# Prompt attention with plain float32 operands, two kv heads per step on halves of the TensorE array

## The chip, the cores and the metric

One core of a Trainium2 chip runs the whole program. The metric is the device time of one execution in microseconds, the median of several. The engines are TensorE (PE for its matmuls, PEld for its weight loads), VectorE (DVE), ScalarE (ACT), GpSimd (POOL) and the engine that issues most loads (SP). Each works through its own queue in order, and waits for the others by semaphores.

## What is computed

The program is a two-layer decoder step for one prompt of 512 tokens and eight short samples. The change concerns the attention of layer 1 for the prompt alone: 16 heads in 4 kv groups, 4 heads to a group, 64 numbers to a head. Each head attends three times (compressed, selected and window branch), each with its own keys and values, and the three outputs are added with gates. With 512 tokens every causal block is selected and the window holds every earlier token, so both of the last two branches are causal attention over 512 keys.

```python
s = jnp.einsum('bqgrd,bngd->bqgrn', qg, ck)                    # compressed, 31 keys
p_cmp = masked_softmax(s, cend[None, None, None, None, :] <= t5)
o_cmp = jnp.einsum('bqgrn,bngd->bqgrd', p_cmp.astype(cv.dtype), cv)
...
s = jnp.einsum('bqgrd,bqgksd->bqgrks', qg, kv_sel[..., 0, :])  # selected
p = masked_softmax(s, m.reshape(B, Q, KV_HEADS, 1, k_sel * SEL_BLOCK))
o_slc = jnp.einsum('bqgrks,bqgksd->bqgrd', p, kv_sel[..., 1, :])
s = jnp.einsum('bqgrd,bmgd->bqgrm', qg, wkv[:, :, 0])          # window
p = masked_softmax(s, wm[None, :, None, None, :])
o_win = jnp.einsum('bqgrm,bmgd->bqgrd', p.astype(wkv.dtype), wkv[:, :, 1])
o = g[..., 0:1] * o_cmp + g[..., 1:2] * o_slc + g[..., 2:3] * o_win
...
return o @ w_o, ...
```

## The kernel before

`prompt_attention` (L1318) runs between sample attention, whose last operations overlap its loads, and `out_proj` (L1558), which multiplies the outputs by `nsa_w_o`. All operands of its matmuls are in a float32 format of one pass (F32R), and accuracy is kept by splitting a number into a high and a low part.

*Operands.* Queries (`queries`, L1402) are loaded by a query head r of all four groups, split by ACT and DVE or POOL into `qhl` with high and low side by side, and transposed so that 64 rows hold the high and 64 rows the low parts (`queries2`). Keys (`load_keys`, `keys`) are loaded twice side by side, four loads a tile plus one for values, transposed, and split into `KSh`, `KSl`, `KWh`, `KWl`; a product of `[qh; ql]` with `[k; k]` over 128 rows then has both query parts. Values become `VP`, high and low as 128 columns.

*Items.* There are 32 items (r, p, e, j): r the query head of a group, group g = 2p + e, j the branch (0 selected, 1 window). `scores_step` makes the causal scores of four query tiles t with 512, 384, 256 and 128 keys, two matmuls each; DVE adds the mask and takes the minimum (L1478), ACT takes the exponential and its sum (L1479), POOL multiplies by gate over sum (L1487). Tile t=0 shares a PSUM bank with another tile. `transpose_step` turns ten 128 x 128 blocks and splits them into `pph` and `ppl` (ACT, then DVE). `values_step` does two matmuls per key tile, adds the compressed branch at j=1 (L1523) and then adds the two column halves of the result (`osum`), splits the sum into `xh` (ACT) and `xl` (POOL).

*Order.* In loop i stand scores of item i, transposes of item i-2 and values of item i-3. A table `plan` sets when a round r prepares the next: query load, transposes, compressed scores (`pk`), their softmax (`ec`) and its transposes (`pct`). The scheduler turns this into a fixed queue on each engine; PSUM has eight banks, all in one pool. `out_proj` fetches the weights in four quarters `rawb1` to `rawb4`, each in four loads of SP, splits each into `whb` (ACT, L247) and `wlb` (DVE, L248), and loads the residual `xz` on ACT's queue. Where a tile lies, and so what a load into it must wait for, is decided by the pools.

Of the kernel before, what the change touches and what calls it, by code (L numbers as in the profile page):

```python
# [20 lines left out]
TP = 512  # L21
# [31 lines left out]
LASTI = (31,)  # L53
LASTT = (0, 1, 2)
B1 = 8
PLA = 2
PB = 4
PT = 2
# [73 lines left out]
def body(tc, top, I, O):  # L132
# [1185 lines left out]
    def prompt_attention(ctx):  # L1318
        gp_ = N["gp"]
        qp = Slots(ctx, "pq", "right", kd=2, vt=2, qs=1, qhl=1)  # L1320
        pa = Slots(ctx, "pa", Q=2)
# [3 lines left out]
        kvs = []  # L1325

        def load_keys(t):
            kd = qp.tile([128, 2, 4, 2, 64], F32, tag="kd", name=f"kd{t}")
            vt = qp.tile([128, 2, 4, 64], F32, tag="vt", name=f"vt{t}")
            for j in range(2):  # L1330
                src = kvd[t * 128:(t + 1) * 128, 1 + j].rearrange("p (k g c) -> p k g c", k=2, g=4)
                for e in range(2):
                    sp.dma_start(kd[:, j, :, e], src[:, 0])
            sp.dma_start(vt.rearrange("p j g c -> p j (g c)"), kvd[t * 128:(t + 1) * 128, 1:3, 256:512])
            kvs.append((kd, vt))

        load_keys(0)
        load_keys(1)
        KS = [pa.tile([128, 4, 512], F32R, name=f"KS{n}") for n in "hl"]
        KW = [pa.tile([128, 4, 512], F32R, name=f"KW{n}") for n in "hl"]  # L1340
        VP = [pa.tile([128, 4, 4, 2, 64], F32R, name=f"VP{j}") for j in range(2)]

        KB = pa.tile([128, 2, 640], F32R, name="KB")
        pool.memset(f32(KB), 0.0)
        cvp = pa.tile([128, 4, 2, 64], F32R, name="cvp")
# [3 lines left out]
        pp.reserve("osum", 2)  # L1349
        for tag in ("pha", "pla", "phb", "plb", "phc", "plc", "pch", "pcl"):  # L1350
            ptp.reserve(tag, PT)
        pool.memset(f32(cvp), 0.0)

        def compressed():
            hs = N["hid"]
            hg_ = ptp.tile([128, TP], F32R, tag="pch", name="hgp").rearrange("p (a k n) -> p a k n", a=2, k=2)
# [6 lines left out]
            ptv = pt[:, :128].rearrange("p (g n) -> p g n", g=4)  # L1363
            kb = KB.rearrange("p a (g n) -> p a g n", g=4)[:, :, :, 0:32]
            b2k = N["b2"][:, 64:65]
            act.activation(kb[:, 0], ptv, AF.Identity, bias=b2k)
            dve.scalar_tensor_tensor(kb[:, 1], ptv, b2k, f32(kb[:, 0]), OP.add, OP.subtract)
# [5 lines left out]
            dve.tensor_tensor(cvf, pt[:, 64:128], cvf, OP.add)  # L1373
            for g in range(4):
                rs = slice(32 * g, 32 * g + 32)
                dve.tensor_copy(cvp[rs, g, 0], cvf[rs])
                dve.tensor_tensor(cvp[rs, g, 1], cvf[rs], f32(cvp[rs, g, 0]), OP.subtract)

        def keys(t):
            if t > 1:  # L1380
                load_keys(t)
            kd, vt = kvs[t]
            for j in range(2):
                pt = tpt(f"pkp{t}{j}")
                for g in range(4):
                    transpose(pt[:, g * 128:(g + 1) * 128], kd[:, j, g].rearrange("p e c -> p (e c)"))
                pv = pt.rearrange("p (g n) -> p g n", g=4)
                hi, lo = ((KS, KW)[j][n][:, :, t * 128:(t + 1) * 128] for n in range(2))
                act.activation(hi, pv, AF.Copy)
                dve.tensor_tensor(lo, pv, f32(hi), OP.subtract)  # L1390
                act.activation(VP[j][:, t, :, 0], vt[:, j], AF.Copy)
                pool.tensor_tensor(VP[j][:, t, :, 1], vt[:, j], f32(VP[j][:, t, :, 0]), OP.subtract)

        keys(0)
        keys(1)
# [7 lines left out]
        def queries(r):  # L1403

            Q[r] = pa.tile([128, 4, TP], F32R, tag="Q", name=f"Q{r}")
            qs = qp.tile([128, 4, 4, 64], F32, tag="qs", name=f"qs{r}")
            for t in range(4):
                sp.dma_start(qs[:, t], qd[t * 128:(t + 1) * 128].rearrange("p (g r c) -> r p g c", g=4, r=4)[r])
            qhl = qp.tile([128, 4, 4, 2, 64], F32, tag="qhl", name=f"qhl{r}")
            act.activation(qhl[:, :, :, 0].bitcast(F32R), qs, AF.Copy)  # L1410
            (pool if r else dve).tensor_tensor(qhl[:, :, :, 1], qs, qhl[:, :, :, 0], OP.subtract)
            gate[r] = gpv[:, :, :, r]
            return qhl

        def queries2(r, qhl):
            for g in range(4):
                pt = tpt(f"pq{r}{g}")
                for t in range(4):
                    transpose(pt[:, t * 128:(t + 1) * 128], qhl[:, t, g].rearrange("p s c -> p (s c)"))
                evac(Q[r][:, g], pt)  # L1420

        def cmp_scores(r):
            pk = mmt(f"pk{r}")
            for n in range(2):
                for g in range(4):
# [28 lines left out]
        def cmp_probs(r, ec):  # L1454
            pt = tpt(f"pct{r}")
            for t in range(4):
                transpose(pt[:, t * 128:(t + 1) * 128], ec[:, t].rearrange("p g n -> p (g n)"))
            pch = ptp.tile([128, TP], F32R, tag="pch", name=f"pch{r}")
            pcl = ptp.tile([128, TP], F32R, tag="pcl", name=f"pcl{r}")
            act.activation(pch, pt, AF.Copy)  # L1460
            dve.tensor_tensor(pcl, pt, f32(pch), OP.subtract)
            cmpp[r] = (pch, pcl)

        items = [(r, p, e, j) for r in range(4) for p in range(2) for e in range(2) for j in range(2)]
        probs, probsT, acc, osum = {}, {}, {}, {}

        def scores_step(i):
            r, p, e, j = items[i]
            g, K = 2 * p + e, (KS, KW)[j]
            P = pp.tile([128, 1280], F32, tag="P", name=f"P{i}")  # L1470
            st = sm.tile([128, 4, 4], F32, tag="st", name=f"st{i}")
            banks = [mmt(f"psp{i}{q}") for q in range(3)]
            views = [banks[1][:, 384:512], banks[2][:, 0:256], banks[1][:, 0:384], banks[0]]
            for t in (3, 2, 0, 1):
                n = (t + 1) * 128
                for hl in range(2):
                    pe.matmul(views[t], Q[r][:, g, t * 128:(t + 1) * 128], K[hl][:, g, 0:n], start=hl == 0, stop=hl == 1)  # L1477
                dve.tensor_tensor_reduce(P[:, tri(t)], views[t], pm[:, 512 - n:512], 1.0, 3e38, OP.add, OP.min, st[:, 1, t:t + 1])  # L1478
                act.activation(P[:, tri(t)], P[:, tri(t)], AF.Exp, bias=st[:, 1, t:t + 1], scale=-1.0, accum_out=st[:, 2, t:t + 1])  # L1479
            dve.reciprocal(st[:, 3], st[:, 2])  # L1480
            dve.tensor_tensor(st[:, 3], st[:, 3], gate[r][:, :, g, 1 + j], OP.mult)
            for t in (3, 2, 0, 1):
                x = P[:, tri(t)]
                if i in LASTI and t in LASTT:
                    dve.tensor_scalar(x, x, st[:, 3, t:t + 1], None, OP.mult)
                else:
                    pool.tensor_tensor(x, x, st[:, 3, t:t + 1].broadcast_to([128, (t + 1) * 128]), OP.mult)  # L1487
            probs[i] = P

        def transpose_step(i):  # L1490
            P = probs.pop(i)
            out = {}
            for name, group in (("a", ((0, 0),)), ("b", ((1, 0), (3, 384))), ("c", ((2, 0),))):
                pt = tpt(f"ppp{i}{name}")
                w = 0
                for kc, c0 in group:
                    for t in range(kc, 4):
                        w = c0 + (t - kc + 1) * 128
                        transpose(pt[:, w - 128:w], P[:, tri(t)][:, kc * 128:(kc + 1) * 128])
                ph = ptp.tile([128, 512], F32R, tag="ph" + name, name=f"pph{name}{i}")  # L1500
                pl = ptp.tile([128, 512], F32R, tag="pl" + name, name=f"ppl{name}{i}")
                act.activation(ph[:, :w], pt[:, :w], AF.Copy)
                dve.tensor_tensor(pl[:, :w], pt[:, :w], f32(ph[:, :w]), OP.subtract)
                for kc, c0 in group:
                    n = (4 - kc) * 128
                    out[kc] = (ph[:, c0:c0 + n], pl[:, c0:c0 + n])
            probsT[i] = out
# [275 lines left out]
```

## Time and profile before

| | us |
|---|---|
| median of 3 runs (1708.69 to 1710.13) | 1709.5 |
| the profiled execution | 1708.67 |
| its span, first to last instruction | 1706.9 |
| sample attention's last transpose starts | 1011.5 |
| first scores of prompt attention | 1024.6 |
| first matmul of the output projection | 1193.2 |

Times in the rows below are microseconds from the start of the span. The granted clock of TensorE over the span is 0.988 of the full level. A timeline row is one instruction, or a run of equal ones, with the idle time ahead of it and what ended that; its length includes the passage through the array, so that lengths of back-to-back matmuls overlap. In the chain of waits each piece lasts until the next one begins, and its pieces add up. A plain float32 matmul leaves two records in the trace, one of F32R one.

### The profile page before, as it was taken

Reading aid. Unit: us, or ns where it says so; the run is one execution under the profiler, and the core shown is the slowest. Engines: PE = TensorE matmul, PEld = TensorE weight load, DVE = VectorE, ACT = ScalarE, POOL = GpSimd, SP = SyncE. Lnnn points to the kernel's source line nnn. Section 1 sums busy time; section 2 is a strip of 40 time slices with the busy share of each in tenths; the row PEclk is TensorE's granted clock in tenths of the full one; section 3 lists DMA queues with packets and bytes.
Section 4 is the critical chain, followed back from the end, with each engine's and each line's share of the span. In section 5 each row is a group of like instructions: output and inputs, shape, how many; then the busy total and the mean of one; then the engine's idle time right before and its main releaser. Section 6 shows DMA issues by size and latency. Waiting matters only on the chain. (4 is left out here: it accounts for less than half of the span.)

```text
span 1706.9 us, 31668 instructions
## 1 busy us (share of the span) xinstructions
PE 1638.8 (96%) x12711; PEld 1555.0 (91%) x12711; DVE 1046.9 (61%) x2162; ACT 816.3 (48%) x1499; POOL 426.5 (25%) x606
## 2 busy tenths in 40 slices
PE   7999999999999989999999988999999999999995
PEld 7999999999999989999956667887999999999995
DVE  7766464545574347889755558898466545454547
ACT  5654334343353314655654447888256534344331
POOL 2222121111020013333312216766023202111104
PEclk9999999999999999999999999999999999999998
DMA  5233132223247736544659941002512222222211
GB/s 190 83 100 100 55 111 83 75 75 99 63 167 214 229 119 244 187 167 164 208 182 350 342 124 26 1 12 69 153 50 75 78 96 75 84 90 81 93 60 56
DMA packets 130850, 206.02 MB, mean 121 GB/s; under 512 B 25775, under 2 KB 106761, under 8 KB 120336
## 3 DMA queue, kind: packets, MB, share of 16 engines
q1 hardware_dynamic: 120800, 134.49, 25.0%
q0 software_dynamic: 9216, 67.11, 11.1%
q8 instruction: 100, 1.64, 0.4%
q10 hardware_dynamic: 688, 2.40, 0.4%
q14 instruction: 46, 0.38, 0.1%
HBM read 179.63 MB, written 24.84 MB: 120 GB/s over the span
## 5 line engine op out<-in xcount | busy, mean ns | idle before, releaser
L168 PE MATMUL u<-xl,wha 128*128 128x288 f32 x704 | 208.0, 296 | 0.3 <-POOL xl L342 0.2
L168 PE MATMUL u<-xl,whb 128*128 128x288 f32 x704 | 208.0, 296 | 0.2
L168 PE MATMUL u<-xh,whb 128*128 128x288 f32 x704 | 207.3, 295 | 0.0
L168 PE MATMUL u<-xh,wha 128*128 128x288 f32 x704 | 207.3, 295 | 0.0
L168 PE MATMUL u<-xh,wlb 128*128 128x288 f32 x704 | 207.3, 295 | 0.0
L168 PE MATMUL u<-xh,wla 128*128 128x288 f32 x704 | 207.2, 295 | 0.0
L408 POOL COPY fcol<-u 128x18 f32<-128x18 f32 x88 | 69.4, 798 | 467.1 <-ACT u L407 467.0
L413 DVE SCALAR_TENSOR_TENSOR c<-u,convp,c 128x592 f32<-128x592 f32 x88 | 72.2, 831 | 122.2 <-ACT c L412 122.2
L248 DVE TENSOR_TENSOR wla<-rawa,wha 128x2048 fp32r<-128x2048 f32 (+1 forms) x52 | 99.5, 1918 | 68.7 <-ACT wha L247 68.0
L248 DVE TENSOR_TENSOR wlb<-rawb,whb 128x2048 fp32r<-128x2048 f32 x37 | 84.8, 2292 | 83.4 <-ACT whb L247 83.4
L168 PEld LDWEIGHTS u<-xl,wha 128*128 128x128 f32 x704 | 132.0, 188 | 2.0 <-DVE xl L342 1.1
L168 PEld LDWEIGHTS u<-xl,whb 128*128 128x128 f32 x704 | 132.0, 188 | 1.9 <-DVE xl L342 1.1
L168 PEld LDWEIGHTS u<-xh,whb 128*128 128x128 f32 x704 | 132.0, 188 | 0.1
L168 PEld LDWEIGHTS u<-xh,wha 128*128 128x128 f32 x704 | 132.0, 188 | 0.1
L168 PEld LDWEIGHTS u<-xh,wlb 128*128 128x128 f32 x704 | 132.0, 188 | 0.0
L168 PEld LDWEIGHTS u<-xh,wla 128*128 128x128 f32 x704 | 132.0, 188 | 0.0
L247 ACT ACTIVATE wha<-rawa 128x2048 fp32r<-128x2048 f32 (+1 forms) x52 | 83.0, 1615 | 91.1 <-PE d L168 58.9
L247 ACT ACTIVATE whb<-rawb 128x2048 fp32r<-128x2048 f32 x37 | 70.9, 1915 | 113.5 <-DMA rawb<-in_ffn_w_up 41.0
L494 DVE SCALAR_TENSOR_TENSOR xz<-xz,d 128x288 f32<-128x288 f32 x160 | 70.1, 450 | 85.5 <-PE d L168 84.8
L901 PE MATMUL pr<-xhi,W1h 128*128 128x256 f32 x512 | 105.6, 288 | 10.2 <-ACT xhi L874 10.2
L874 ACT ACTIVATE xhi<-xf 128x1024 fp32r<-128x1024 f32 (+1 forms) x68 | 70.1, 1031 | 83.1 <-PE pr L901 46.0
L168 PE MATMUL d<-hh,wha 128*128 128x288 f32 x352 | 104.4, 298 | 0.1
(779 smaller groups left out, 4900.6 us busy)
## 6 DMA issues: line engine op xcount, KB each, us to landing
rawa<-in_ffn_w_up SPq DMA_DIRECT2D x22, 1024.0 KB
rawb<-in_ffn_w_up SPq DMA_DIRECT2D x22, 1024.0 KB
rawa<-in_ffn_w_down SPq DMA_DIRECT2D x11, 1024.0 KB
rawb<-in_ffn_w_down SPq DMA_DIRECT2D x11, 1024.0 KB
rawa<-in_nsa_w_in SPq DMA_DIRECT2D x9, 1024.0 KB
sr<-in_state_win_kv SPq DMA_DIRECT2D x8, 1024.0 KB
out_win_kv_s<-sr SPq DMA_DIRECT2D x8, 1008.0 KB
rawb<-in_nsa_w_o SPq DMA_DIRECT2D x16, 256.0 KB
```

The costliest lines, as they stand in the source:

```text
L168: pe.matmul(out, a, b, start=first and j == 0, stop=last and j == n - 1)
L247: act.activation(h[:, a:b], r[:, a:b], AF.Copy)
L248: dve.tensor_tensor(lo[:, a:b], r[:, a:b], f32(h[:, a:b]), OP.subtract)
L408: pool.tensor_copy(col[:, :, m].rearrange("p (j i) -> p j i", i=2), u[:, TP:TP + 90].rearrange("p (j i) -> p j i", i=10)[:, :, 0:2])
L413: dve.scalar_tensor_tensor(c, u[:, 1:1 + CW], cv[:, 44 + m:45 + m], c, OP.mult, OP.add)
L494: dve.scalar_tensor_tensor(z, z, ALPHA if first else 1.0, p_[:, :HALF], OP.mult, OP.add)
L874: act.activation(xhi.rearrange(flat), xf.rearrange(flat), AF.Copy)
L901: pe.matmul(banks[b, kv][ri][:, :, gh * nn:(gh + 1) * nn], W1[wi][:, kv, ri * 8 + th * 4 + c], xx[:, c // 2, c % 2].rearrange("p g n -> p ...
```

## The change

The matmuls of the attention take plain float32 operands, without parts. One step does both groups e = 0, 1 of a pair p, so there are 16 steps (r, p, j).

- Scores: keys and queries of two groups lie in the two halves of the 128 rows (`KT`, `Q`), and each group's matmul uses 64 rows, one matmul per (t, e), in different PSUM banks, six banks a step.
- Values: each group's matmul uses 64 of the array's columns and writes its half of one bank, `po`; values are read straight from the loaded tile `kvt`. The compressed branch likewise; the outputs are split from `po` itself, high part on ACT, low part on DVE.
- Compressed scores: four matmuls on quarters of the columns, instead of eight on the whole array.
- Transposes of P stay ten per item, each block copied once (DVE a, a, c; ACT b, b, c of a step).
- Loads: four whole-row loads `kvt` for keys and values, no duplicates, and no split of queries. 8 transposes of queries a round instead of 16, 16 of keys instead of 32.
- Six buffers of P instead of four, four of the transposed instead of two; one step of look-ahead. In the last step DVE and POOL share the multiplies.

The core of the diff:

```diff
-        qp = Slots(ctx, "pq", "right", kd=2, vt=2, qs=1, qhl=1)
-        pa = Slots(ctx, "pa", Q=2)
+        qp = Slots(ctx, "pq", "right", qs=2)
+        pa = Slots(ctx, "pa", QT=2)
...
+        for t in range(4):
+            x = pa.tile([128, 2, 512], F32, name=f"kvt{t}")
+            sp.dma_start(x, kvd[t * 128:(t + 1) * 128, 1:3])
+            kvt.append(x)
+        KT = pa.tile([128, 2, 2, TP], F32, name="KT")
...
         def cmp_scores(r):
             pk = mmt(f"pk{r}")
-            for n in range(2):
-                for g in range(4):
-                    pe.matmul(pk, KB[:, n, 128 * g:128 * g + 128], Q[r][:, g], start=n == 0 and g == 0, stop=n == 1 and g == 3)
+            for g in range(4):
+                pe.matmul(pk[32 * g:32 * g + 32], KB[:, g], Q[r][:, g // 2], start=True, stop=True, tile_position=(0, 32 * g))
...
         def scores_step(i):
-            r, p, e, j = items[i]
-            g, K = 2 * p + e, (KS, KW)[j]
...
-            banks = [mmt(f"psp{i}{q}") for q in range(3)]
-            views = [banks[1][:, 384:512], banks[2][:, 0:256], banks[1][:, 0:384], banks[0]]
             for t in (3, 2, 0, 1):
                 n = (t + 1) * 128
-                for hl in range(2):
-                    pe.matmul(views[t], Q[r][:, g, t * 128:(t + 1) * 128], K[hl][:, g, 0:n], start=hl == 0, stop=hl == 1)
...
+                for e in range(2):
+                    if t:
+                        bank = mmt(f"psp{i}{e}{t}")
+                        views[e, t] = bank[:, 0:n]
+                        if t == 2:
+                            views[e, 0] = bank[:, 384:512]
+                    rs = slice(64 * e, 64 * e + 64)
+                    pe.matmul(views[e, t], Q[r][rs, p, t * 128:(t + 1) * 128], KT[rs, j, p, 0:n], start=True, stop=True)
...
         def transpose_step(i):
...
-                act.activation(ph[:, :w], pt[:, :w], AF.Copy)
-                dve.tensor_tensor(pl[:, :w], pt[:, :w], f32(ph[:, :w]), OP.subtract)
+                    if name == "b" or (name == "c" and e):
+                        act.activation(ph[:, :w], pt[:, :w], AF.Copy)
+                    else:
+                        dve.tensor_copy(ph[:, :w], pt[:, :w])
...
         def values_step(i):
...
-                v = VP[j][:, kc, g].rearrange("p a c -> p (a c)")
-                for q, x in enumerate(pT[kc]):
-                    pe.matmul(po[:, kc * 128:], v, x, start=j == 0 and kc == 0 and q == 0, stop=False)
+                for e in range(2):
+                    g = 2 * p + e
+                    pe.matmul(po[64 * e:64 * e + 64, kc * 128:], kvt[kc][:, j, 256 + 64 * g:320 + 64 * g], pT[e][kc],
+                              start=j == 0 and kc == 0, stop=False)
             if j == 1:
-                act.activation(o, po[64:128], AF.Copy)
-                dve.tensor_tensor(o, po[0:64], o, OP.add)
...
+                for e in range(2):
+                    pe.matmul(po[64 * e:64 * e + 64], cvp[:, 2 * p + e], cmpp[r], start=False, stop=True)
+                act.activation(oh[:, c, 0:TP], po, AF.Copy)
+                dve.tensor_tensor(ol[:, c, 0:TP], po, f32(oh[:, c, 0:TP]), OP.subtract)
...
-        for i in range(len(items) + LA + 1):
+        for i in range(len(items) + 2):
```

*Order of PE.* Before, in the first round: `psp31` is item 3's bank for t=2 and t=0, `psp32` its bank for t=1, `ppp1` are the transposes of item 1.

```order
L1477 MATMUL psp31_12452<-KWh_12062,Q0_12196 128x384
L1477 MATMUL psp31_12452<-KWl_12066,Q0_12196 128x384
L1477 MATMUL psp32_12453<-KWh_12062,Q0_12196 128x256
L1477 MATMUL psp32_12453<-KWl_12066,Q0_12196 128x256
L1477 MATMUL psp21_12391<-KSh_12054,Q0_12196 128x128
L1477 MATMUL psp21_12391<-KSl_12058,Q0_12196 128x128
L200 MATMUL ppp1a_12476<-cst_58,P1_12344 128x128 x4
L200 MATMUL ppp1b_12485<-cst_58,P1_12344 128x128 x4
L200 MATMUL ppp1c_12494<-cst_58,P1_12344 128x128 x2
L1477 MATMUL psp31_12452<-KWh_12062,Q0_12196 128x128
L1477 MATMUL psp31_12452<-KWl_12066,Q0_12196 128x128
L200 MATMUL pct0_12501<-cst_58,ec0_12376 128x128 x4
```

Now, step 9 (`psp902`: step 9, group e=0, bank of t=2; its second row is t=0), followed by the transposes of step 8 for e=0 (`ppp80`):

```order
L1451 MATMUL psp903_13123<-KT_12048,Q2_12776 128x512
L1451 MATMUL psp913_13125<-KT_12048,Q2_12776 128x512
L1451 MATMUL psp902_13131<-KT_12048,Q2_12776 128x384
L1451 MATMUL psp912_13133<-KT_12048,Q2_12776 128x384
L1451 MATMUL psp901_13145<-KT_12048,Q2_12776 128x256
L1451 MATMUL psp902_13131<-KT_12048,Q2_12776 128x128
L1451 MATMUL psp911_13147<-KT_12048,Q2_12776 128x256
L1451 MATMUL psp912_13133<-KT_12048,Q2_12776 128x128
L198 MATMUL ppp80a_13165<-cst_58,P80_13014 128x128 x4
L198 MATMUL ppp80b_13172<-cst_58,P80_13014 128x128 x4
L198 MATMUL ppp80c_13179<-cst_58,P80_13014 128x128 x2
```

Before, the ten transposes of another item stand between an item's score matmuls of t=1 and that of t=0; now the matmuls of t=0 follow directly, with one of t=1 between them.

*Order of SP* around the loads of the output weights (`rawb`) and of a state of the last feed-forward part (`fst1`). Before:

```order
L1408 DMA qs3_13588<-qd_71 128x4x64 x4
L1569 DMA rawb1_14660<-in_nsa_w_o 64x4x256 x4
L1569 DMA rawb2_14669<-in_nsa_w_o 64x4x256 x4
L378 DMA fst1_15280<-in_state_ffn 128x5x128
L1569 DMA rawb3_14678<-in_nsa_w_o 64x4x256 x4
L1569 DMA rawb4_14847<-in_nsa_w_o 64x4x256 x4
```

Now:

```order
L1382 DMA qs3_13105<-qd_71 128x4x64 x4
L376 DMA fst1_14582<-in_state_ffn 128x5x128
L377 DMA fst1_14582<-in_state_ffn 64x128
L1539 DMA rawb1_13962<-in_nsa_w_o 64x4x256 x4
L1539 DMA rawb2_13971<-in_nsa_w_o 64x4x256 x4
L1539 DMA rawb3_13980<-in_nsa_w_o 64x4x256 x4
```

The state load, which waits for the last but one step's values, stood behind two quarters of the weights and stands ahead of all four.

## Rows read from the trace of the kernel before

**Rows 1.** Stretches: length, PE, PEld, DVE, ACT, POOL busy (instructions), clock, DMA share, GB/s
```profile
1040.00:1060.00 20.00, 18.22 (x106) 16.33 (x105) 15.03 (x50) 14.04 (x40) 12.49 (x16) 0.83 0.09 21
1060.00:1080.00 20.00, 18.56 (x122) 16.08 (x122) 18.44 (x61) 17.79 (x51) 13.13 (x17) 1.00 0.03 7
```

**Rows 2.** Timeline: first score matmul of items 0, 6, 30, 31: start, us, what [idle]
```profile
1024.57 0.68 PE L1477 MATMUL psp<-KSh,Q 128*128 128x512 f32 x2 [0.25 <-ACT KSh L1389]
...
1058.11 0.40 PE L1477 MATMUL psp<-KSh,Q 128*128 128x512 f32 x1
...
1175.79 0.39 PE L1477 MATMUL psp<-KSh,Q 128*128 128x512 f32 x1
...
1180.11 0.39 PE L1477 MATMUL psp<-KWh,Q 128*128 128x512 f32 x1
```

**Rows 3.** Timeline of PE before the first scores
```profile
1011.52 0.30 PE L200 MATMUL pot<-cst,osb 128*128 128x128 f32 x1 [1.24 <-DVE osb L1277]
...
1017.64 2.02 PE L200 MATMUL pkp<-cst,kd 128*128 128x128 f32 x8 [3.14 <-DMA kd<-kvd]
1020.04 3.40 PE L200 MATMUL pq<-cst,qhl 128*128 128x128 f32 x16 [0.38 <-DVE qhl L1411]
```

**Rows 4.** Chain of waits in the same stretch: start, us, what (x pieces)
```profile
1010.31 1.37 SPq L1408
...
1018.67 1.24 DVE qhl L1411
```

**Rows 5.** Chain of waits in the steady part, PE
```profile
1055.57 1.44 PE pk L1426 x6
1057.01 1.26 PE pop L1519 x8
...
1059.32 0.44 PE ppp4a L200 x4
...
1096.15 1.43 PE pk L1426 x6
...
1136.27 1.44 PE pk L1426 x6
```

**Rows 6.** Chain of waits in the steady part: multiplies, exponentials, score reads
```profile
1143.73 3.20 POOL P L1487 x4
1146.94 1.26 POOL ec L1446
...
1153.32 2.29 ACT P L1479 x8
...
1165.50 0.60 DVE P L1478
...
1166.11 0.47 DVE P L1478
```

**Rows 7.** Chain of waits in sample attention: plain float32 on column halves
```profile
961.21 1.01 PE pss L1099 x4
...
963.02 1.90 PE po L1269 x32
```

**Rows 8.** Timeline of PE at the selector: row quarters, 8 records
```profile
793.36 0.42 PE L1150 MATMUL psb<-sel,cst 32*128 32x34 f32 x8
```

**Rows 9.** Timeline of PE in the start
```profile
1045.32 0.63 PE L1477 MATMUL psp<-KSh,Q 128*128 128x512 f32 x1
```

**Rows 10.** Chain of waits around the end of the attention
```profile
1186.09 4.82 DMA rawb<-in_nsa_w_o
...
1191.28 1.81 ACT whb L247
...
1193.11 2.30 DVE wlb L248
...
1197.40 7.99 DMA rawb<-in_nsa_w_o
```

**Rows 11.** Timeline of PE where the output projection starts
```profile
1195.46 0.40 PE L168 MATMUL wo<-xh,wlb 128*128 128x288 f32 x1 [1.53 <-DVE wlb L248]
```

More of the change, by code (lines that the diff above doesn't have):

```diff
@@ L52 @@
 NP = ((0,), (1,), (2,), (), (3, 4, 5, 6), (7, 8, 9, 10))
-LASTI = (31,)
 LASTT = (0, 1, 2)
 B1 = 8
-PLA = 2
-PB = 4
-PT = 2
+PB = 6
+PT = 4
 SR = 5
@@ L1319, in prompt_attention @@
         gp_ = N["gp"]
-        qp = Slots(ctx, "pq", "right", kd=2, vt=2, qs=1, qhl=1)
-        pa = Slots(ctx, "pa", Q=2)
+        qp = Slots(ctx, "pq", "right", qs=2)
+        pa = Slots(ctx, "pa", QT=2)
         pp = Slots(ctx, "pp")
         ptp = Slots(ctx, "pt")
[L1325 to L1345, printed above, removed]
+        kvt = []
+        for t in range(4):
[3 more added lines that the diff above has]
+        KT = pa.tile([128, 2, 2, TP], F32, name="KT")
+        KB = pa.tile([128, 4, 32], F32, name="KB")
+        cvp = pa.tile([128, 4, 64], F32, name="cvp")
+        pool.memset(KB, 0.0)
+        pool.memset(cvp, 0.0)
         pp.reserve("ks", 1)
@@ L1348, in prompt_attention @@
         pp.reserve("P", PB)
-        pp.reserve("osum", 2)
-        for tag in ("pha", "pla", "phb", "plb", "phc", "plc", "pch", "pcl"):
+        for tag in ("pta", "ptb", "ptc"):
             ptp.reserve(tag, PT)
-        pool.memset(f32(cvp), 0.0)
+        ptp.reserve("pc", 2)
+        hgp = pa.tile([128, TP], F32R, name="hgp")
         def compressed():
             hs = N["hid"]
-            hg_ = ptp.tile([128, TP], F32R, tag="pch", name="hgp").rearrange("p (a k n) -> p a k n", a=2, k=2)
+            hg_ = hgp.rearrange("p (a k n) -> p a k n", a=2, k=2)
             hg = [hg_[:, n] for n in range(2)]
@@ L1372, in compressed @@
             dve.tensor_tensor(cvf, pt[:, 0:64], N["b2"][:, 0:64], OP.add)
-            dve.tensor_tensor(cvf, pt[:, 64:128], cvf, OP.add)
             for g in range(4):
                 rs = slice(32 * g, 32 * g + 32)
-                dve.tensor_copy(cvp[rs, g, 0], cvf[rs])
-                dve.tensor_tensor(cvp[rs, g, 1], cvf[rs], f32(cvp[rs, g, 0]), OP.subtract)
+                dve.tensor_tensor(cvp[rs, g], pt[rs, 64:128], cvf[rs], OP.add)
         def keys(t):
-            if t > 1:
-                load_keys(t)
-            kd, vt = kvs[t]
+            pt = tpt(f"pkp{t}")
             for j in range(2):
-                pt = tpt(f"pkp{t}{j}")
-                for g in range(4):
[L1386 to L1395, printed above, removed]
+                for p in range(2):
+                    k = 2 * j + p
+                    transpose(pt[:, k * 128:(k + 1) * 128], kvt[t][:, j, p * 128:(p + 1) * 128])
+            evac(KT[:, :, :, t * 128:(t + 1) * 128], pt.rearrange("q (j p n) -> q j p n", j=2, p=2))
         sm = mkpool(ctx, "pp4", 8)
@@ L1457, in cmp_probs @@
                 transpose(pt[:, t * 128:(t + 1) * 128], ec[:, t].rearrange("p g n -> p (g n)"))
[L1458 to L1465, printed above, removed]
@@ L1467, in scores_step @@
-        def scores_step(i):
-            r, p, e, j = items[i]
-            g, K = 2 * p + e, (KS, KW)[j]
-            P = pp.tile([128, 1280], F32, tag="P", name=f"P{i}")
-            st = sm.tile([128, 4, 4], F32, tag="st", name=f"st{i}")
-            banks = [mmt(f"psp{i}{q}") for q in range(3)]
-            views = [banks[1][:, 384:512], banks[2][:, 0:256], banks[1][:, 0:384], banks[0]]
+            cmpp[r] = ptp.tile([128, TP], F32, tag="pc", name=f"pc{r}")
+            evac(cmpp[r], pt)
+        items = [(r, p, j) for r in range(4) for p in range(2) for j in range(2)]
@@ L1474, in scores_step @@
+        probs, probsT, acc = {}, {}, {}
+        def scores_step(i):
+            r, p, j = items[i]
+            P = [pp.tile([128, 1280], F32, tag="P", name=f"P{i}{e}") for e in range(2)]
+            st = [sm.tile([128, 4, 4], F32, tag="st", name=f"st{i}{e}") for e in range(2)]
+            views = {}
             for t in (3, 2, 0, 1):
                 n = (t + 1) * 128
-                for hl in range(2):
-                    pe.matmul(views[t], Q[r][:, g, t * 128:(t + 1) * 128], K[hl][:, g, 0:n], start=hl == 0, stop=hl == 1)
@@ L1478, in scores_step @@
[L1478 to L1487, printed above, removed]
+                for e in range(2):
[4 more added lines that the diff above has]
+                            views[e, 0] = bank[:, 384:512]
+                    rs = slice(64 * e, 64 * e + 64)
+                    pe.matmul(views[e, t], Q[r][rs, p, t * 128:(t + 1) * 128], KT[rs, j, p, 0:n], start=True, stop=True)
@@ new lines, in scores_step @@
+                for e in range(2):
+                    x, s_ = P[e][:, tri(t)], st[e]
+                    dve.tensor_tensor_reduce(x, views[e, t], pm[:, 512 - n:512], 1.0, 3e38, OP.add, OP.min, s_[:, 1, t:t + 1])
+                    act.activation(x, x, AF.Exp, bias=s_[:, 1, t:t + 1], scale=-1.0, accum_out=s_[:, 2, t:t + 1])
+            for e in range(2):
+                s_ = st[e]
+                dve.reciprocal(s_[:, 3], s_[:, 2])
+                dve.tensor_tensor(s_[:, 3], s_[:, 3], gate[r][:, :, 2 * p + e, 1 + j], OP.mult)
+                for t in (3, 2, 0, 1):
+                    x = P[e][:, tri(t)]
+                    if i == len(items) - 1 and (e == 1) == (t in LASTT):
+                        dve.tensor_scalar(x, x, s_[:, 3, t:t + 1], None, OP.mult)
+                    else:
+                        pool.tensor_tensor(x, x, s_[:, 3, t:t + 1].broadcast_to([128, (t + 1) * 128]), OP.mult)
@@ L1507, in transpose_step @@
-            probsT[i] = out
+            for e, P in enumerate(probs.pop(i)):
+                out = {}
+                for name, group in (("a", ((0, 0),)), ("b", ((1, 0), (3, 384))), ("c", ((2, 0),))):
+                    pt = tpt(f"ppp{i}{e}{name}")
+                    w = 0
+                    for kc, c0 in group:
+                        for t in range(kc, 4):
+                            w = c0 + (t - kc + 1) * 128
+                            transpose(pt[:, w - 128:w], P[:, tri(t)][:, kc * 128:(kc + 1) * 128])
+                    ph = ptp.tile([128, 512], F32, tag="pt" + name, name=f"pph{name}{i}{e}")
+                    if name == "b" or (name == "c" and e):
+                        act.activation(ph[:, :w], pt[:, :w], AF.Copy)
+                    else:
+                        dve.tensor_copy(ph[:, :w], pt[:, :w])
+                    for kc, c0 in group:
+                        out[kc] = ph[:, c0:c0 + (4 - kc) * 128]
+                probsT[i, e] = out
@@ L1509, in values_step @@
         def values_step(i):
-            r, p, e, j = items[i]
-            g = 2 * p + e
+            r, p, j = items[i]
             if j == 0:
-                acc[i] = mmt(f"pop{i}")
-            po = acc[i] if j == 0 else acc.pop(i - 1)
-            pT = probsT.pop(i)
+                acc[r, p] = mmt(f"pop{i}")
+            po = acc[r, p]
+            pT = [probsT.pop((i, e)) for e in range(2)]
             for kc in (0, 1, 3, 2):
-                v = VP[j][:, kc, g].rearrange("p a c -> p (a c)")
-                for q, x in enumerate(pT[kc]):
-                    pe.matmul(po[:, kc * 128:], v, x, start=j == 0 and kc == 0 and q == 0, stop=False)
+                for e in range(2):
+                    g = 2 * p + e
+                    pe.matmul(po[64 * e:64 * e + 64, kc * 128:], kvt[kc][:, j, 256 + 64 * g:320 + 64 * g], pT[e][kc],
+                              start=j == 0 and kc == 0, stop=False)
@@ L1520, in values_step @@
             if j == 1:
-                cv = cvp[:, g].rearrange("p a c -> p (a c)")
-                for q, x in enumerate(cmpp[r]):
-                    pe.matmul(po, cv, x, start=False, stop=q == 1)
-                if e == 0:
-                    osum[r, p] = pp.tile([128, TP], F32, tag="osum", name=f"osum{r}{p}", bufs=2)
-                o = osum[r, p][64 * e:64 * e + 64]
-                act.activation(o, po[64:128], AF.Copy)
-                dve.tensor_tensor(o, po[0:64], o, OP.add)
-                if e == 1:
-                    c = 4 * p + r
-                    act.activation(oh[:, c, 0:TP], osum[r, p], AF.Copy)
-                    pool.tensor_tensor(ol[:, c, 0:TP], osum[r, p], f32(oh[:, c, 0:TP]), OP.subtract)
@@ L1534, in prompt_attention @@
-        qhl = queries(0)
+                for e in range(2):
+                    pe.matmul(po[64 * e:64 * e + 64], cvp[:, 2 * p + e], cmpp[r], start=False, stop=True)
+                c = 4 * p + r
+                act.activation(oh[:, c, 0:TP], po, AF.Copy)
+                dve.tensor_tensor(ol[:, c, 0:TP], po, f32(oh[:, c, 0:TP]), OP.subtract)
+        q0 = queries(0)
         compressed()
-        keys(2)
-        queries2(0, qhl)
-        keys(3)
+        for t in range(4):
+            keys(t)
+            if t == 0:
+                queries2(0, q0)
```

64 lines of the change are left out of this document (21 added, 43 removed).

## The prediction

> **What bounds the kernel now.** The change stays inside one stage of some 180 us, prompt attention, so that stage is read. First the table by stretches [rows 1]: in the steady part PE and DVE are each busy about 18.5 of 20 us, ACT 17.8, POOL 13. No engine is so idle that the gain of another counts in full. Then the starts of the first score matmul of an item, one head group and one branch, of which there are 32 [rows 2]: item 0 at 1024.57, item 6 at 1058.11, item 30 at 1175.79, item 31 at 1180.11. The output projection waits last at 1195.46, its first matmuls having started at about 1193.2 (1195.46 less the wait of 1.53 and four matmuls) [rows 11]. That gives four pieces: a prologue after sample attention, whose last transpose on PE starts at 1011.52 [rows 3]; the start, 33.5 us for six items; the middle, 117.7 us for 24 items; and the tail, 17.4 us from item 30 on. The middle is not even. A round of eight items takes 40.6 and 40.1 us between the three starts of a round's compressed scores [rows 5], while the last items, which have no such extras beside them, are 4.32 us apart [rows 2]: two are 8.65 us, and a round's extras (queries, compressed scores and softmax) cost some 5.7 us. PE's own sum of a round is about 35: per item 1.26 for scores (as many columns as values), 1.1 for ten transposes, 1.26 for values and 0.24 for compressed values, eight times, and 1.9 and 24 transposes of extras [rows 5].
>
> **The prologue.** Before, five small loads per key tile go through SP's queue and the first query load starts behind them, at 1010.31. PE stands 3.14 us for keys and runs 24 transposes in 2.02 + 3.40 us; the queries wait for a split that DVE starts at 1018.67, behind a string of small compressed-value operations [rows 3, 4]. Afterwards the four whole-row key loads are issued while sample attention still runs, the queries need no split, and PE has 24 transposes in all (16 of keys, 8 of queries) and five compressed matmuls. At 0.11 us each [rows 5] that is 3.2 us, plus one copy at the end, as long as a score read of as many columns, 0.6 [rows 6]: from 1011.5 to 1015.4. I take 1016.0, **8.5 us** earlier, with 6 (copies on ACT and DVE lie late) and 10 as bounds.
>
> **A step of the middle.** A step does two heads, so it stands against two items. PE's parts come from matmuls on plain float32 halves, which sample attention already has:
> - A pair of 512 columns on column halves takes 1.01 us for both, and eight pairs of 128 columns 1.90 [rows 7]. One pass over 512 columns is four transposes, 0.44 us [rows 5]; two passes for both together are 0.88, so the halves run side by side, and some 0.13 us go into the change to and from the halved array. Row halves of this width are not in the trace; nearest is a selector on row quarters, whose 8 records fit into 0.42 us [rows 8]. By that the row halves run together too; in turn, each pair would take twice as long.
> - Values: 1280 columns of both heads are ten blocks of two passes at 0.11, 2.2 us. Before, an item takes 1.26 [rows 5], two 2.5: 0.3 gained. Compressed values, every second step, 0.88 against four matmuls at 0.24: nothing.
> - Scores: 2.2 too by PE alone, against 2.5. But the order puts t=0 into the bank of t=2, behind DVE's read of it, and no other item's transposes stand between any more (order of PE, above). First pair ready 1.0 after the start, then DVE 0.60 + 0.60 + 0.47 [rows 6]: t=0 of the first head can start at 2.7, of the second 0.47 later, and scores end at 3.5. PE stands some 1.3 us a step; queued behind that wait are the step's 20 transposes and the values.
> - 20 transposes at 0.11: 2.2, as before. Three changes of mode at 0.13: 0.4.
>
> The sum is 3.5 + 2.2 + 2.2 + 0.45 (half of 0.88) + 0.4 = 8.75. Where a step follows an output, DVE's subtraction there stands ahead of the first score read and delays it by about 0.4, 0.2 on average; as much of the mode changes lies under the t=0 wait. So **8.75 us a step**, against 8.65 for two items: the halves win 0.6, and the bare wait and the mode changes take it back. The other engines are hidden: per step ACT has eight exponentials (2 x 2.29 [rows 6]) and 1.2 of copies, DVE 3.3 of score reads and 1.5 of copies, POOL eight multiplies (2 x 3.2 [rows 6]), 5 to 6.5 us each. They lose more than PE, since the splits of P, three operations an item on DVE, are gone.
> Extras: the splits of keys and queries go; a round keeps 16 transposes, 1.8, and compressed scores are one set of 1.0 instead of 1.9; with changes of mode 3.0, plus 1.0 for POOL's two compressed multiplies of 1.26 [rows 6], which push the second head's multiplies back. Twelve steps are 105, three rounds less what falls into the start 11: **116** against 117.7, 1.5 gained. Bounds of the step: 8.1 (the t=0 wait half hidden) to 9.4 (0.6 lost to the other engines, as a round now loses 5 against PE's sum).
>
> **Start and tail.** In the start, three steps against six items, PE waits for POOL and DVE, and then runs at the lower of its two clock levels, 1.2 GHz: 512-column matmuls of 0.63 us at 1045.32 [rows 9] instead of 0.40 at 1058.11 [rows 2], granted clock 0.83 in the mean of 1040 to 1060 [rows 1]. DVE's queue there held splits between the softmax rows; afterwards none. Two score steps back to back; exponentials until 6.2, POOL 3.2 per head until 12 to 13; transposes, the third scores and their softmax rows to about 19; transposes and values to 25. I take **25** against 33.5, 8.5 gained, bounds 5 and 11. The tail holds scores 3.5, transposes 2.2, values 3.1, a wait for the last multiplies of about 1.5, transposes 2.2, values 2.2 and 3.1, of which 0.8 lies in that wait: **17**, 0.4 gained.
>
> **The weights behind it.** This is the loss. Before, the first quarter of the output weights is long there, and PE loses about 2.2 at 1193.2 to 1195.46, 1.53 of it idle, to the splits [rows 11]. The new order of SP puts a state load, which waits for the values of the last step but one, ahead of the first quarter (order of SP, above), and where the pools now put the tiles, the second quarter and the split weights lie in key and value tiles that the last values read. So the first quarter is issued some 3 us before the end of the values, its last part at about the end; it lands 4.82 later [rows 10], less one part's issue, at 4; ACT 1.81 and DVE 2.30 [rows 10] make 8.2, where before PE runs in full at 2.2: 6.0 lost. Behind such an idle stretch PE runs at 1.2 GHz: after 3.14 us idle, sixteen transposes took 3.40 instead of 1.8, and the eight before them 2.02 instead of 0.9 [rows 3]: 2.5 more. **8.5 us lost.** Low end 3 (the values further apart, full clock); high end 16, if the residual's load on the same rings makes the first two quarters take 7.99 each [rows 10] instead of 4.82.
>
> **Sum.** -8.5 - 8.5 - 1.5 - 0.4 + 8.5 = -10.4 against the profiled execution of 1708.67 (span 1706.9, 1.8 outside it): 1698.3. The median of the runs shown is 0.8 higher, 1709.5: **1699**.
>
> **A rule of the Trainium skill.** The rows show 1.01 us for a 512-column pair on column halves. The Trainium skill, TensorE: Matmul & The Clock Gate, section Packing small matmuls, reports a gain of 3.07 from four row tiles, about a quarter short of four; by that, an estimate, a pair of passes would take 1.15 instead of 0.88, some 1.3 us a step, and the sum would be near +10. The rows of this case speak against it for column halves; none shows 64-row halves.
>
> **Rivals.**
> - *Halves in turn.* If matmuls of the row halves do not overlap, or the column halves stop doing so where waits pull the pairs apart, values cost 2.2 more a step, scores 0.9 to 2.2 (part lies under the t=0 wait), compressed values 0.4: 3.5 x 16 = 56, 1755. For it: no row of 64-row halves. Against: [rows 7, 8]. From a loss of 0.65 us a step on (10.4 / 16), 15% of what overlaps, it decides the sign; in part it ends slower, from 1713 up. The Trainium skill's rule above (Packing small matmuls) would be this one in part, at about 1719.
> - *Given back.* Steps of 9.2 (0.45 x 16 = 7) or the weights at their high end (7.5): 1706; both, 1713. For it: before, a round takes 40.3 where PE's sum is 35, so such sums run short.
> - *The relief counts.* If DVE and ACT run ahead, the t=0 wait halves and the extras cost PE's part alone: twelve steps at 8.1 and 3 less: 1688.
>
> **How the numbers follow.** Forecast 0.45 (1692 to 1705), relief 0.17 (1682 to 1692), given back 0.22 (1705 to 1714), halves in turn 0.16 (above 1713). The range 1684 to 1714 leaves out the far part of the relief and the slower case. 0.2%, 3.4 us, is about what a measurement of this kernel can tell from no change. Below 1706.1: 0.45 + 0.17 + 0.06 = 0.68; within: 0.14; above 1712.9: 0.16 + 0.02 = 0.18.
>
> **What would show it.** Right: first scores near 1016; the two row-half matmuls of a pair starting within some ns of one another; a step without extras of 8.5 to 9.0 us, with PE waits on DVE's score read of over 1 us; values 2.2 to 2.4; output matmuls that wait for the first quarter's load and split 6 to 10 us after the last values, and then run slower at first. Wrong: second heads that start a full pass later, steps over 9.4 or under 8.2, weights there before the last values, or a start that still takes 30 us.

## The result and the profile after

The changed kernel takes 1719.4 us (median of 6, 1717.9 to 1721.3) against 1709.8 for the kernel before (median of 6): a ratio of 1.0054, 95% interval 1.0040 to 1.0069. It is slower by half a percent, clear of noise, where 1699 was forecast. The profiled execution took 1718.37, its span 1716.6, 9.7 us longer than before.

By the pieces of the prediction, in us (starts from the timelines of PE; the values end, before, at 1193.2, where the first output matmul starts, and after, at 1192.6: the start of the last four value matmuls, 1191.73, plus the 0.86 that four of them take in the chain of waits):

| piece | before | forecast | after |
|---|---|---|---|
| first scores at | 1024.57 | 1016.0 | 1016.65 |
| start, to step 3 (item 6) | 33.5 | 25 | 25.8 |
| middle, 12 steps (24 items) | 117.7 | 116 | 133.1 |
| tail, to the end of the values | 17.4 | 17 | 17.1 |
| end of the values to the end of the span | 513.7 | 522.2 | 524.0 |

The timeline of PE gives the starts of steps 0, 3, 10 and 15 (start, length, tile, and in brackets what PE waited for); they answer to [rows 2]:

```profile
1016.65 0.70 PE L1451 MATMUL psp<-KT,Q 64*128 64x512 f32 x2 [1.65 <-DVE KT L207]
...
1042.48 0.70 PE L1451 MATMUL psp<-KT,Q 64*128 64x512 f32 x2
...
1123.24 0.70 PE L1451 MATMUL psp<-KT,Q 64*128 64x512 f32 x2
...
1175.54 2.20 PE L1451 MATMUL psp<-KT,Q 64*128 64x512 f32 x10
```

Four of five pieces came as worked out, or within 2 us. The middle is 17 us longer than forecast. Its twelve steps are, from the same timeline: 9.94, **15.60**, 10.27, 9.72, 9.94, **15.04**, 10.27, 9.72, 9.94, **14.53**, 9.39, 8.72. One step in each round is 5 us longer than its neighbours, and it is the one in which the next round's compressed softmax runs. The chain of waits through the second of them (start, length, what):

```profile
1094.36 1.14 POOL P L1465 x2
...
1096.15 4.13 POOL P L1465 x6
1100.28 1.23 POOL ec L1418
1101.51 0.02 issue
1101.53 0.69 DVE cst L1419
1102.22 0.60 DVE xl L1503
1102.81 0.08 DVE cst L1420
1102.90 0.59 DVE P L1454
...
1103.66 0.55 DVE P L1454
...
1104.31 0.47 DVE P L1454
...
1104.84 0.79 PE psp L1451 x2
```

Read from the end: PE's matmul of t=0 waits for DVE's read of t=2 (L1454); DVE's three reads stand in its queue behind a row sum of the softmax (`cst`, L1419); that waits for POOL's mask multiply (`ec`, L1418); and that stands on POOL behind all eight multiplies of P. The score matmuls of t=3 to t=1 had been through by about 1100. The waits of DVE between 1056 and 1180 before, and between 1042 and 1176 after, have this edge in one row each (total us, times, longest):

```profile
DVE cst L1447 <- POOL ec L1446: 0.5, 3, 0.2
```

```profile
DVE cst L1419 <- POOL ec L1418: 11.6, 3, 3.9
```

PE's waits in the middle are then one row. The stretches (length, busy PE, PEld, DVE, ACT, POOL, granted clock, DMA share, GB/s) of a long step and of an ordinary one, and then of the whole middle before and after, show that PE also falls to the lower clock:

```profile
PE psp L1451 <- DVE st L1454: 22.2, 12, 4.7
```

```profile
1098.00:1113.00 15.00, 10.31 (x60) 6.92 (x58) 7.21 (x28) 7.25 (x22) 6.92 (x10) 0.77 0.00 1
...
1123.00:1133.00 10.00, 9.01 (x64) 5.01 (x62) 7.01 (x24) 6.78 (x21) 4.71 (x9) 1.00 0.01 2
```

```profile
1058.11:1175.79 117.68, 110.32 (x722) 96.77 (x721) 105.47 (x347) 103.77 (x291) 84.18 (x110) 1.00 0.07 14
```

```profile
1042.48:1175.54 133.06, 110.85 (x707) 69.48 (x705) 87.00 (x307) 76.67 (x242) 73.25 (x102) 0.94 0.00 1
```

PE is idle for 22.2 us of the middle (length less busy PE) where it was 7.4 before, and that is nearly all of the 15 us by which it has grown. Its busy time is the same, at a granted clock of 0.94 instead of 1.00: by an estimate from these two rows (0.06 of 133 us) the lower clock takes back up to 8 us that the matmuls would have gained.

At the end the weights come late, as forecast, and a little later still. The chain of waits and the timeline of PE, with the stretches at the two clock levels, answer to [rows 10, 11]:

```profile
1191.65 8.37 DMA rawb<-in_nsa_w_o
...
1200.13 1.92 ACT whb L245
...
1202.13 2.31 DVE wlb L246
```

```profile
1191.73 1.03 PE L1500 MATMUL pop<-pc,cvp 128*64 128x512 f32 x4
1202.09 0.61 PE L166 MATMUL wo<-xh,whb 128*128 128x288 f32 x1 [9.34 <-ACT whb L245]
...
1204.48 0.61 PE L166 MATMUL wo<-xh,wlb 128*128 128x288 f32 x1 [1.06 <-DVE wlb L246]
...
1208.24 0.38 PE L166 MATMUL wo<-xh,wlb 128*128 128x288 f32 x1
1208.46 0.29 PE L166 MATMUL wo<-xh,whb 128*128 128x288 f32 x1
```

```profile
1202.00:1208.00 6.00, 4.85 (x18) 4.50 (x19) 2.29 (x1) 1.95 (x2) 0.00 (x0) 0.50 0.49 103
1210.00:1216.00 6.00, 6.00 (x48) 6.00 (x47) 3.05 (x4) 1.92 (x1) 0.00 (x0) 1.00 0.60 117
```

So the account is: first scores -7.9, start -7.7, middle +15.4, tail -0.3, behind the values +10.3: +9.8, against 9.7 in the spans.

### The profile page after: what moved, and what is told of

Same layout as the page of the kernel before. It is cut to its first block, busy times and chain, and to the rows that moved or that the text cites. A ratio compares the mean times of both kernels' runs of the same rounds, so it can differ in the third digit from the quotient of the medians.

```text
span 1716.6 us, 31241 instructions
## 1 busy us (share of the span) xinstructions
PE 1632.3 (95%) x12663; PEld 1512.8 (88%) x12663; DVE 1011.4 (59%) x2088; ACT 771.0 (45%) x1412; POOL 400.1 (23%) x586
## 4 chain that ended last, share of the span: by engine, by line
PE 51%; DVE 4%; issue 3%; POOL 2%; ACT 2%; DMA 1%; SPq 0%; ACTq 0%; POOLq 0%; DVEq 0%
PE u L166 16%; PE pr L899 11%; PE d L166 6%; PE wo L166 3%; PE po L1267 2%; PE pss L1097 2%; PE pk L198 2%; PE pop L1496 2%; PE ppt L198 1%; PE psp L1451 1%; POOL P L1465 1%; DVE P L1454 1%; DMA rawb<-in_nsa_w_o 0%; DVE xn L1576 0%; ACT P L1455 0%
## 5 line engine op out<-in xcount | busy, mean ns | idle before, releaser
L1465 POOL TENSOR_TENSOR P<-P,st 128x512 f32<-128x512 f32 (+3 forms) x124 | 86.9, 732 | 80.0 <-DVE st L1459 21.3
```

What stands on the lines that cost most here:

```text
L1465: pool.tensor_tensor(x, x, s_[:, 3, t:t + 1].broadcast_to([128, (t + 1) * 128]), OP.mult)
```

## Experiments

Theory: three separate causes, DVE's queue behind POOL's mask multiply, the t=0 matmuls behind DVE's read, and the late first quarter of the weights. The rivals are in the expectations. All kernels are edits of the changed one, but for the last. Each was timed beside the kernel before (medians of 1708.0 to 1710.5 there), and "ratio" is its time to that kernel's; gains over the changed kernel are differences of medians that were not taken side by side. By the ratios the first three edits gain 11, 9 and 15 us where the medians say 8.5, 8.4 and 14.5, so some 3 us of such a gain are open.

**The mask multiply on DVE.**

```diff
-            (pool if r else dve).tensor_tensor(ec, ec, cm1, OP.mult)
+            dve.tensor_tensor(ec, ec, cm1, OP.mult)
```

> The changed kernel, but the mask multiply of the compressed softmax (L1418) runs on DVE in every round, not on POOL. Theory: in the three long steps (15.60, 15.04, 14.53 us between score starts, steps 4, 8 and 12 to the next) DVE's queue stands still for 3.87 us, because its row sum waits for this multiply and the multiply stands behind eight multiplies of P on POOL; the score reads of the next step stand behind it, and PE waits 4.7 us and falls to the lower clock. Then DVE waits only for ACT's exponential, about 1 us, and does 0.7 us of multiply: each long step becomes 11 to 12.5 us, PE's longest wait falls from 4.7 to about 2.5, and the time falls by 7 to 12, to 1708 to 1712. Rival: these steps are long because DVE and ACT have too much work in them. Then one more operation on DVE makes them no shorter: 14.5 or more each, 1718 to 1722.

Measured: 1710.9, ratio to before 0.9989 (0.9972 to 1.0007), 8.5 us under the changed kernel. The time lies in the range expected, and the rival is out: one more operation on DVE made the steps shorter. DVE's wait for POOL's `ec` is gone, and the middle takes 126.5 us in the profiled execution, 6.6 less. The long steps are 10.72, 13.71 and 13.86, and the longest wait of PE is 2.31. Only the first is as short as expected. The timeline of PE and the stretches of the first and second long step tell why:

```profile
1057.79 0.49 PE L1451 MATMUL psp<-KT,Q 64*128 64x128 f32 x2 [2.31 <-DVE st L1454]
...
1098.53 0.79 PE L1451 MATMUL psp<-KT,Q 64*128 64x128 f32 x2 [2.31 <-DVE st L1454]
```

```profile
1053.00:1064.00 11.00, 8.69 (x60) 5.54 (x60) 8.76 (x30) 6.61 (x21) 6.30 (x9) 1.00 0.01 2
1094.00:1107.00 13.00, 10.70 (x54) 7.51 (x54) 8.15 (x29) 7.18 (x22) 6.42 (x10) 0.74 0.01 1
```

The wait is the same to 0.01 us, and of these two only the second has the lower clock behind it: those 3 us are the clock's. The third long step, from 1137.50 to 1151.36, has a granted clock of 0.75, like the second. So a long step's surplus of 5 us in the changed kernel is in part wait and in part the lower clock behind it.

**t=0 with t=2.** The score matmuls of t=0 are issued right behind those of t=2, before DVE reads the bank.

```diff
-            for t in (3, 2, 0, 1):
-                n = (t + 1) * 128
-                for e in range(2):
...
+            for ts in ((3,), (2, 0), (1,)):
+                for t in ts:
+                    n = (t + 1) * 128
+                    for e in range(2):
...
+                        pe.matmul(views[e, t], Q[r][rs, p, t * 128:(t + 1) * 128], KT[rs, j, p, 0:n], start=True, stop=True)
+                for t in ts:
+                    n = (t + 1) * 128
+                    for e in range(2):
...
+                        dve.tensor_tensor_reduce(x, views[e, t], pm[:, 512 - n:512], 1.0, 3e38, OP.add, OP.min, s_[:, 1, t:t + 1])
```

> The changed kernel, but the score matmuls of t=0 are issued right behind those of t=2, before DVE reads that bank. Theory: PE's wait for DVE's read of t=2 (0.9 us shown and more in the pair behind it, in nearly every step, 27.0 us in all with the long steps) counts in full; then ordinary steps shrink by 0.9 to 1.3, from 9.7 to 10.3 down to 8.6 to 9.2, and the time falls by 11 to 17, to 1703 to 1708. Rival: other engines or PSUM banks set the pace of a step, and the wait moves to the transposes; then steps shrink by under 0.3 and the time is 1715 to 1720.

Measured: 1711.0, ratio 1.0003 (0.9989 to 1.0017), 8.4 under the changed kernel and above the range expected. The ordinary steps did shrink, to 7.00 to 9.40 (mean of the nine 8.61, before the edit 9.77), so the wait counts in the steps. But the long steps stay at 14.60, 14.22 and 12.74, since there the wait only moved, to the transposes behind the scores: DVE still waits for POOL's mask multiply, 14.4 us in the three instead of 11.6, and the transposes for DVE. The timeline of PE in the second:

```profile
1102.52 1.12 PE L198 MATMUL ppp70b<-cst,P 128*128 128x128 f32 x4 [3.11 <-DVE xl L1506]
```

The middle takes 119.1 us, 14.0 less. But part of that was lost elsewhere: the start, from step 0 to step 3, takes 29.6 us instead of 25.8, at a granted clock of 0.83 instead of 1.00, and the wait for the weights is 11.8 instead of 9.3.

**Early weights.** A tile that nothing uses shifts the pools, so that the first two quarters get memory of their own.

```diff
+        hole = mkpool(ctx, "hole").tile([128, 2, 2048], F32, name="hole")
         qp = Slots(ctx, "pq", "right", qs=2)
```

> The changed kernel, but the first two quarters of the output weights get SBUF of their own: a tile of 16 KB per partition that nothing uses is put ahead of the key tiles, and the quarters come to lie there, so that their loads need not wait for the last score and value matmuls. Theory: the late first quarter costs 9 to 10 us: 9.34 of wait and 1.06 behind it, and a stretch at the lower clock, against 2.4 of wait before the change. Then output matmuls run in full within 2 to 4 us of the last values and the time falls by 7 to 10, to 1709 to 1712. Rival: split and residual load hold PE as long anyway; the wait stays over 6 us and the time is 1716 or more.

Measured: 1704.9, ratio 0.9965 (0.9947 to 0.9983), 14.5 under the changed kernel; more than expected. The attention is as before the edit (steps within 0.1 us), and the output projection follows the last values at once. In the chain of waits:

```profile
1191.23 0.86 PE pop L1501 x4
1192.09 7.97 PE wo L166 x59
```

From the last value matmul's start to the last output matmul's it is 56.5 us, against 69.5 in the changed kernel and 59.0 before the change. So 13 us lie here, of which 2.5 are waits that the kernel before had too. The expectation had priced only the return to the kernel before.

**All three.**

> All three edits together. Theory: three separate causes, so the gains add: 25 to 36 us less than the changed kernel, 1684 to 1694, and faster than the kernel before by 15 to 25. Rival: the waits cover for one another (a step without its t=0 wait runs into the next of POOL or DVE); then the gains add to less than 20, 1700 or more.

Measured: 1683.6 (1682.9 to 1685.5), ratio 0.9834 (0.9813 to 0.9856): 27 us faster than the kernel before and 36 faster than the changed one, just past the range expected. The rival, that the waits cover for one another, is out. The gains of the single edits add up to 31.4 by the medians and 35 by the ratios, against 36 and 38 together: no surplus clear of noise. The start still takes 29.7 us at a granted clock of 0.83, as with the second edit alone. The long steps are 11.29, 9.09 and 9.09, the middle 108.2 us against 117.7 before and 133.1. The second long step, and the longest of what is left of PE's waits from 1042 to 1153:

```profile
1091.00:1100.00 9.00, 7.82 (x58) 4.85 (x56) 7.75 (x30) 6.73 (x21) 5.65 (x8) 1.00 0.01 2
```

```profile
PE ppp111b L198 <- DVE st L1458: 0.7, 1, 0.7
PE ppp71b L198 <- DVE st L1458: 0.7, 1, 0.7
PE ppp31b L198 <- DVE st L1458: 0.6, 1, 0.6
```

**Two of three.** The second and third edit without the first, and the first and third without the second.

> The second and third edit without the first (the mask multiply stays on POOL). The three edits alone were worth 8.5, 8.4 and 14.5 us, together 36: 5 more than their sum. Theory: in a long step the wait for POOL and the wait for t=0 stand in one chain, and either alone is still long enough that TensorE falls to the lower clock behind it; so the mask multiply is worth more once the t=0 wait is gone. Then this kernel is 1694 to 1698, long steps 12.5 to 14.5, 10 to 14 above the kernel with all three. Rival: the surplus of 5 us comes from the weights alone (a faster attention made their wait longer); then it is 1690 to 1693.

Measured: 1692.5, ratio 0.9901 (0.9881 to 0.9922); long steps 13.50, 13.30 and 13.74. By the medians the mask multiply is worth 8.9 on top of the other two, much as it is alone. The time lies in the rival's range, 1.5 us below the theory's, and the long steps lie in the theory's; with an interval of 7 us from end to end this does not tell the two apart.

> The first and third edit without the second (t=0 still behind DVE's read of t=2). Theory: the long steps keep a wait of 2.3 us and in part the lower clock, the ordinary ones keep 0.9 to 1.4 of wait: 1694 to 1699, 11 to 15 above the kernel with all three. Rival: with the weights early, the t=0 wait alone is worth its 8.4 us: 1691 to 1693.

Measured: 1697.9, ratio 0.9936 (0.9914 to 0.9958); long steps 10.72, 10.72 and 13.77. The time lies in the theory's range and not in the rival's. The t=0 order is worth 14.3 on top of the other two and 8.4 alone, so its worth grows; part of that is the weights' wait, which grows by 2.5 when it comes alone. Intervals of some 3 us to either side leave the rest open.

**The first step shared.** The largest wait left with all three edits is in the start.

```diff
-                    if i == len(items) - 1 and (e == 1) == (t in LASTT):
+                    if i in (0, len(items) - 1) and (e == 1) == (t in LASTT):
```

> All three edits, and the multiplies of the first step are shared by DVE and POOL as those of the last are. With the three edits PE's longest wait left is 3.22 us for POOL at the first transposes, where POOL does eight multiplies in 5.5 us alone, and behind it PE runs at the lower clock until about 1034 (granted clock 0.80 from 1020 to 1040). Theory: the wait halves, the clock stays up, and the 13.61 and 12.69 us of the second and third step become 10 to 12 each: 3 to 6 us less than with the three edits, 1678 to 1681. Rival: DVE, which then also does the score reads of the second step, takes the place of POOL; no change beyond 1 us.

Measured: 1684.9, ratio 0.9865 (0.9849 to 0.9882), no gain. The second step got shorter, 11.25 instead of 13.61, and the third longer, 14.71 instead of 12.69; DVE is busy 18.9 of the 20 us from 1020 to 1040, against 14.9 without this edit. PE's longest wait for POOL at the first transposes fell only from 3.2 to 2.4. The rival held: DVE takes POOL's place.

**The kernel before, with t=0 behind t=2.**

> The kernel before the change, with its score matmuls of t=0 right behind those of t=2, as in the second edit. Theory: there the transposes of another item hide most of this wait (4.9 us in all in the steady part), and DVE and ACT are near full, so little comes of it: 0 to 5 us faster, 1705 to 1710, far from what the changed kernel reaches with its three edits. Rival: the wait weighs as much there, and the old operands would be as fast with the same order: 1695 or less.

Measured: 1706.1 against 1708.0 on the same chip, ratio 0.9985 (0.9975 to 0.9995). There the same order is worth 2 to 3 us. There was little to win: with the transposes of another item in between, PE waited 4.9 us for score reads between 1056 and 1180, against 22.2 in the changed kernel's middle. So with all three edits the changed operands are 22 us (by medians) to 26 us (by ratios) ahead of the old ones with that same order. Some 2.5 us of that are the early weights (59.0 against 56.5, above), which were not tried on the kernel before.

## Why the prediction was wrong

1. *The prologue* was right: 1016.65 for 1016.0, the copies last (PE waits 1.65 for `KT`).
2. *The step* was right in its mechanism and 0.3 short. The row at 1123.24 above holds the first records of both heads' matmuls over 512 columns; each lasts 0.69 us and both together 0.70, so they start within 0.01 us of each other. The row halves run side by side, and the rival of halves in turn is out. The page TensorE: Matmul & The Clock Gate of the Trainium skill, section Packing small matmuls, describes tiles that start within some ns of each other and overlap; the trace agrees, with these 0.70 us. Steps without extras are 9.39 and 8.72, mean 9.05, for 8.75. The t=0 wait is there, but mis-sized: PE idles 0.80 to 0.99 us in an ordinary step, not 1.3, and the scores last 4.1 in the step below, not 3.5. The wait also pulls the pairs of t=1 and t=0 apart, which the 2.2 for the scores did not count. The same stretch in an ordinary step of the second edit, where all pairs stay together, lasts 2.36:

```profile
1126.43 0.96 PE L1451 MATMUL psp<-KT,Q 64*128 64x128 f32 x6 [0.99 <-DVE st L1454]
1127.33 0.66 PE L198 MATMUL ppp90a<-cst,P 128*128 128x128 f32 x4
```

```profile
1110.61 2.43 PE L1452 MATMUL psp<-KT,Q 64*128 64x512 f32 x16
1112.97 0.66 PE L198 MATMUL ppp80a<-cst,P 128*128 128x128 f32 x4
```

3. *The extras of a round* are the step that failed: "1.0 for POOL's two compressed multiplies of 1.26 [rows 6], which push the second head's multiplies back". A round takes 44.97 (15.04 + 10.27 + 9.72 + 9.94), where 4 x 8.75 + 3.0 + 1.0 = 39.0 was worked out: 6.0 too little. Over the twelve steps it is 133.1 against 116 (the sum took a gain of 1.5 for 117.7 less 116; that changes nothing). The multiply was priced by what it delays on POOL, with DVE called hidden. What counts is who waits for it and what stands behind that one: DVE's row sum, with all score reads of the next step behind it, and PE behind those. [rows 6] held the piece: POOL's `ec` of 1.26 directly behind four multiplies in the chain. Before the change two heads' multiplies came in two bursts of four, and DVE waited 0.2 at most; now there are eight in a row, and DVE waits 3.87. The first edit shows it: the wait goes, and with it 6.6 us of the middle and 8.5 of the time. The rest of the 17 us is the t=0 wait, which stands in the same long steps, and the clock behind both: with the second edit too, in the kernel with all three, the middle takes 108.2 (the third edit alone leaves the steps as they are).
4. *The clock* was counted at the end and in the start, not in the long steps. The granted clock is 0.78, 0.77 and 0.88 in the three. Where it falls, that is some 2 to 3.5 us a time, by these shares (what is missing to 1, times the length of the step) and by the two equal waits of the first edit.
5. *Start and tail* were right: 25.8 for 25 and 17.1 for 17.
6. *The weights* were right in mechanism and 1.8 short: 10.3 for 8.5. The first quarter took 8.37 to land, not 4.82: the row of 7.99, which stood at the high end, was the nearer one. The residual's four loads are issued ahead of it, from 1183 to 1188, and the DMA engines are full meanwhile (share 1.12 and 1.15 from 1192 to 1200), so they share the time; no run moves the residual alone. Of the 10.3 some 8.0 are the waits (9.34 + 1.06 against 1.53 + 0.90 before), and the rest fits the clock of 0.50.

The slower rival that was named, halves in turn, did not happen. The time of about 1719 that went with its milder form is the one that was measured, but that is luck: the middle is long mainly by three steps of some 5 us too much, and the row halves run side by side. The right rival, a wait that takes the place of the relief, was named only as steps of 9.2. On average they are 11.1.

## What to carry to other kernels

When two steps are merged into one, each engine's burst doubles, and whatever stood between two bursts now stands behind one: look through the queues for a small operation whose result another engine waits for, and price it by what is queued behind the waiter, not by its own length. A tile that reads and writes one PSUM bank by turns wants its writes issued together, before the first read, as soon as no other work stands between. And memory that a stage frees late is a wait for the next stage's loads: a tile of 16 KB a partition that holds nothing was worth 14 us.

## What was not expected of the hardware

The same wait of 2.31 us on PE, in the same place of two equal rounds of one execution, went with a granted clock of 1.00 in its step once and of 0.74 the next time, 3 us apart in the length of the step. What decides between the two no run here shows. The spread of a kernel from run to run goes with the clock: the ten runs of the first edit go from 1705.9 us at a granted clock of 0.986 over the span to 1715.4 at 0.980, the five of the first and third edit from 1694.8 at 0.989 to 1701.3 and 1701.4 at 0.985.
